# Starting the sparse stage with the blocks that need no key selection, and gating outputs out of PSUM

## The chip, the cores and the metric

The kernel runs on one core of one Trainium2 chip. The metric is device time in microseconds for one execution of the whole layer. TensorE (PE), VectorE (DVE), ScalarE (ACT), GpSimd (POOL) and the DMA queues, of which SyncE (SP) issues most, run at the same time, each through its own instruction stream in a fixed order, and wait for one another through semaphores. TensorE's granted clock stands at one of two levels, 1.2 or 2.4 GHz; a stretch's mean is given as a share of full speed.

## What is computed

One layer of a decoder over 1024 tokens of width 1024: a half-step feed-forward, two attention mixers side by side on the same normalised input, a gated merge, and a second half-step feed-forward. The part that matters here, cut from the reference:

```python
# (a) sparse attention, 128 queries at a time; top_k = 256
score = einsum('bths,bth->bts', relu(dots), wi)            # causal, else -inf
_, idx = lax.top_k(score, top_k)
logits = einsum('bthd,btkd->bthk', qa, kg) * HEAD_DIM**-0.5 # over the chosen keys
p = softmax(where(valid, logits, -inf))
y_a = einsum('bthc,hcd->bthd', einsum('bthk,btkc->bthc', p, vg), w_uv)
# (b) stick-breaking attention
log_a = log_sigmoid(z) + (reverse_cumsum(log_not) - log_not)
y_b = einsum('bhts,bshd->bthd', where(strict, exp(log_a), 0), v_b)
# merge
merged = sigmoid(g_a) * (y_a @ w_oA) + sigmoid(g_b) * (y_b @ w_oB)
x = x + merged @ w_out
```

A query block i of 128 tokens sees (i + 1) * 128 keys. Blocks 0 and 1 see at most 256, so every causal key is chosen there and no selection is made; blocks 2 to 7 need one.

## The kernel before, in words

Products are made in two parts, high and low, so that a product of full accuracy takes three matmuls (`mm3`), a logit or value product two or three. Between the two feed-forwards the order of the work is not written out: each piece is a generator (a stream) that yields what it needs next, an engine first, then tiles, rings of buffers or named marks. A planner (`Weave`) holds a cost for each instruction, picks the stream that can go earliest (a lower rank wins a tie), and so fixes the order of TensorE, VectorE, ScalarE and GpSimd. `when` says at which planned time a list of needs is fulfilled. SP's queue is ordered apart from it.

The stretch that the change touches is the planner's run named "attend". Its streams, with their ranks on TensorE: `values` (0), `sticks` (1), `head_values` (2), `latent_values` (3), `logits` (4), `outputs` (6), and the filling projections of gates that are left over (7). Also `topk`, one stream for the group of blocks 7, 2, 3 (mark `top0`) and one for 4, 5, 6 (mark `top1`): a bit-by-bit search for the 256th score, by signs counted on ScalarE, and then per block comparisons, a scan and a bias row of 0 and -1e30, stored by GpSimd into `bd`.

`sticks` makes the products `psz` of a head's query block, ScalarE two sigmoids, VectorE a scan (L1534) and a product (L1537). `values` turns them by transposes (`pstT`) copied out by ScalarE and VectorE (`turned_out`, L1581 and L1583), multiplies by the values (`psy`), and stores `y_b` (`ybhd`, `ybld`). At its end it waits for both marks `top0` and `top1`, closes the places `sw` and `ss` (the memory of scores and stick rows), and spawns `sparse`.

`sparse` opens the place `sc` there: three gate tiles, two more rows for `e`, six `o` tiles, and the value-up weight. It clears a raw tile on VectorE (L1657), loads the weight's eight heads through SP (L1660), and makes its high part on ScalarE (L1662) and its low part on GpSimd (L1664). The mark `c` says that the places are open, `uv` that the weight is there.

The sparse blocks go in the order `blocks = (5, 4, 7, 6, 3, 2, 1, 0)`. For each, `latent_queries` loads the queries through SP, `hidden_keys` loads the bias through SP (for blocks 0 and 1 GpSimd makes it), `logits` makes eight heads' products `psL` (L1723, L1724), VectorE adds the bias and takes the maximum (L1685, L1692), ScalarE the exponential (L1697), VectorE the normalising (L1699, L1700). The rows `e` lie in four tiles `a1`, two `left` and two `e`, taken in a fixed turn of eight heads. `latent_values` transposes four heads at a time (`pspT`, L1778) and multiplies by the latent values (`pso`, L1758 to L1760). `o_out` splits the result into two `o` tiles; `head_values` multiplies a pair of blocks by the value-up weight (`psya`), gives back its four `o` tiles, and marks `ya0` to `ya3`.

`outputs` projects: 16 units `ob` of y_b (eight weight pieces of 128 rows by two halves of the tokens), whose gated results go to `obd`, and eight units `oa` of y_a for tokens 512 to 1023, which add `obd` and go to `md`. A unit is twelve matmuls of 512 columns. For both, `gated` lets ScalarE copy the bank out (L1836), GpSimd multiply by the gate (L1841) and, for `oa`, add the other part (L1844), and GpSimd issue the store (L1845). `gate_load` loads the gate (L1828) and the other part (L1831) through SP, into a ring of three tiles; evictions share a ring `evr` of three.

After the run, the second half of the layer begins with the eight units `psm` for tokens 0 to 511, in new PSUM banks: VectorE multiplies by the gate out of PSUM (L1913), adds (L1914), and GpSimd makes low parts of weight pieces (L291) as it did in the run before (L962).

Of the kernel before, what the change touches and what calls it, by code (L numbers as in the profile page):

```python
# [93 lines left out]
class Weave:  # L94
# [94 lines left out]
    def when(self, needs, eng):  # L189
        t = 0.0  # L190
        for n in needs:
            if isinstance(n, str):
                t = max(t, self.when(self.marks[n], eng) if n in self.marks else float("inf"))
            elif isinstance(n, Stream):
                t = max(t, float("inf") if n.end is None else n.end)
            elif isinstance(n, (Ring, tuple)):
                ring, count = n if isinstance(n, tuple) else (n, 1)
                for old in ring.live[:max(len(ring.live) + count - ring.bufs, 0)]:
                    old = old.tensor.name
                    t = max(t, float("inf") if self.held[old] else self.done[old] + self.HOP)  # L200
            elif n is not None and not isinstance(n, (int, float)):
                t = max(t, self.ready[n.tensor.name] + self.hop(n.tensor.name, eng))
        return t
# [39 lines left out]
def trunk(ctx, tc, x, positions, g_ffn1, w1_gate, w1_up, w1_down, g_mix, w_in, g_cq, w_uq_a, w_q_idx,  # L243
# [664 lines left out]
    with fp as fpool, fps as fpsum, psm as psum, tc.manual_schedule(  # L908
# [271 lines left out]
        def heads():  # L1180
# [14 lines left out]
            for n, (nm, d) in enumerate((("kkh", kad[0]), ("kkl", kad[1]), ("kkh", vad[0]), ("kkl", vad[1]))):  # L1195
                yield SP, here[nm][n // 2]
                KV.append(here[nm][n // 2](nm))
                nc.sync.dma_start(f32(KV[-1]), d)
            mark("kv", *KV)

        def latent_queries():
            for n, i in enumerate(blocks):
                ring = here["qs"][n % 2]
                yield SP, "kv", ring
# [4 lines left out]
        blocks = (5, 4, 7, 6, 3, 2, 1, 0)  # L1209
# [304 lines left out]
        s = place("sw", "right")  # L1514
        here["x2"] = ring_of(s, "x2", 3, dt=F16)
# [107 lines left out]
        def values():  # L1623
# [18 lines left out]
            yield PE, *products, "top0", "top1"  # L1642
            yield PE, *outs
            s.close()
            keep.close()
            spawn(sparse())

        def sparse():
            c = here["c"] = place("sc", "right")
            here["gate"], here["e"] = ring_of(c, "gate", 3, (P, 512)), ring_of(c, "e", 2)  # L1650
            here["o"] = ring_of(c, "o", 6, dt=F32R)

            raw = here["e"]("uvraw")
            UV.extend((c("uvh", "uvh", 1, F32R), c("uvl", "uvl", 1, F32R)))
            mark("c")
            yield DVE
            nc.vector.memset(raw, 0.0)  # L1657
            for h in range(H):
                e = h % 2
                nc.sync.dma_start(raw[:, h * P + e * HD:h * P + (e + 1) * HD], w_uv_a[0, h])  # L1660
            yield ACT, raw
            nc.scalar.activation(UV[0], raw, AF.Copy)  # L1662
            yield POOL, raw, UV[0]
            nc.gpsimd.tensor_tensor(UV[1], raw, f32(UV[0]), op=ALU.subtract)  # L1664
            give(raw)
            mark("uv", UV[1])

        def hidden_keys():
            for b, i in enumerate(blocks):
                nk = (i + 1) * P  # L1670
                yield (SP if i >= 2 else POOL), biases, "top0", "top1"
# [30 lines left out]
        def logits():  # L1702
            n = 0
            yield PE, "sparse", "kv"
            kah, kal = KV[:2]
            for b, i in enumerate(blocks):
# [3 lines left out]
                for h in range(H):  # L1710
                    k = n % 8
                    if k > 5:
                        yield PE, "c"
                    ring = arings[1] if k < 4 else lefts if k < 6 else here["e"]
                    yield PE, ring
# [26 lines left out]
        def latent_products(b, g, pts, outs):  # L1742
            i = blocks[b]
            vah, val = KV[2:]
            if b % 2 == 0:
                yield PE, wbank, (here["o"], 2)
                OT[i // 2, g] = here["o"](f"oh{g}"), here["o"](f"ol{g}")
# [18 lines left out]
        def latent_values():  # L1766
            n, outs, products = 0, [], []
            yield PE, "c", "kv"
# [64 lines left out]
        def gated(ps, load, row, half, to):  # L1833
# [5 lines left out]
            gate, *other = here["gate", row, half]  # L1839
            yield POOL, o, gate  # L1840
            nc.gpsimd.tensor_tensor(o, o, gate, op=ALU.mult)  # L1841
            for t in other:
                yield POOL, o, t
                nc.gpsimd.tensor_tensor(o, o, t, op=ALU.add)  # L1844
            put_low(to, o)  # L1845
            give(o, gate, *other)

        def project(nm, rows, halves, outs):

            for d in range(0, ND, 2):  # L1850
# [3 lines left out]
                for e in range(2):  # L1854
                    for half in halves:
# [10 lines left out]
                        outs.append(spawn(gated(ps, coming, row, half, to)))  # L1866
                give(*W.parts)

        def outputs():
# [4 lines left out]
            yield SP, "uv"  # L1874
            for p in range(4):
                nc.sync.dma_start(f32(ybh[p]), ybd[0][p * P:(p + 1) * P, :])
                nc.sync.dma_start(f32(ybl[p]), ybd[1][p * P:(p + 1) * P, :])
            outs = []
            yield from project("ob", (ybh, ybl), range(2), outs)
            mark("obd", *outs)  # L1880
            yield PE, "ya1"
# [9 lines left out]
        here["c"].close()  # L1891
        rows_.close()
# [160 lines left out]
```

## Time and profile before

| what | value |
|---|---|
| median of 3 runs | 2324.99 us (2324.81 to 2325.76) |
| the profiled execution's own time | 2321.91 us |
| its span | 2320.1 us |
| TensorE busy, share of the span | 2190.6 us, 94% |
| VectorE | 1577.2 us, 68% |
| ScalarE | 1114.3 us, 48% |
| GpSimd | 901.1 us, 39% |

Busy times are those of instructions; a matmul's end is modelled and neighbouring matmuls overlap, so that the pace of matmuls is read from start to start. Stretches are told in microseconds from the span's start. The change lies between about 1240 and 1565 us.

### The profile page before, as it was taken

How to read it: one execution, taken by the hardware profiler on the slowest of the kernel's cores; microseconds unless marked ns; L12 is line 12 of the kernel's file. 1: busy time of each engine (PE TensorE's matmuls, PEld its weight loads, DVE VectorE, ACT ScalarE, POOL GpSimd, SP SyncE). 2: the span in 40 equal slices, each digit the busy share in tenths (PEclk: the TensorE clock that was granted, in tenths of full speed). 3: DMA queues.
4: the chain of work that ended last, by engine and by line, in shares of the span. 5: the costliest groups of instructions: out<-in, count | busy, mean ns of one | idle time of the engine just before them, and what ended most of it. 6: DMA issues, size and time to landing. Idle time of an engine off the chain costs nothing.

```text
span 2320.1 us, 30206 instructions
## 1 busy us (share of the span) xinstructions
PE 2190.6 (94%) x10460; PEld 1814.1 (78%) x10460; DVE 1577.2 (68%) x2497; ACT 1114.3 (48%) x2138; POOL 901.1 (39%) x659
## 2 busy tenths in 40 slices
PE   7999999999998999899898499989999999999999
PEld 6788888888888877777676388767878888888877
DVE  5766666688771698466788787833476666667685
ACT  4323233344462368998988365633332333233443
POOL 3555555332353344211111022266445555542233
PEclk9999999999999999999999699999999999999999
DMA  5233333587754433655455222457323333358755
GB/s 165 79 117 96 109 96 109 178 312 240 185 173 129 122 105 105 155 126 109 103 125 178 89 88 72 163 168 263 118 69 96 109 100 105 98 168 291 239 166 182
DMA packets 251497, 330.64 MB, mean 143 GB/s; under 512 B 19536, under 2 KB 154336, under 8 KB 251344
## 3 DMA queue, kind: packets, MB, share of 16 engines
q1 hardware_dynamic: 234224, 288.83, 41.4%
q0 software_dynamic: 7488, 24.16, 2.8%
q10 hardware_dynamic: 9632, 15.73, 2.0%
q8 instruction: 82, 1.34, 0.3%
q14 instruction: 71, 0.58, 0.1%
HBM read 234.78 MB, written 93.88 MB: 142 GB/s over the span
## 4 chain that ended last, share of the span: by engine, by line
PE 69%; DVE 10%; issue 7%; ACT 7%; DMA 4%; POOL 2%; ACTq 0%; SPq 0%; DVEq 0%; POOLq 0%
PE p L671 5%; PE p L672 5%; PE p L670 5%; PE pc L461 3%; PE pc L463 3%; PE pc L462 3%; PE pd L463 3%; PE pd L461 3%; PE pd L462 3%; PE pa L463 3%; PE pa L461 3%; PE pa L462 3%; ACT junka L1118 3%; PE pb L463 2%; PE pb L461 2%
## 5 line engine op out<-in xcount | busy, mean ns | idle before, releaser
L1118 ACT ACTIVATE junka<-u,cand,sig 128x1024 bf16<-128x1024 f32 (+5 forms) x186 | 182.5, 981 | 14.8 <-DVE cand L1115 4.7
L1534 DVE TENSOR_TENSOR_SCAN left<-left 128x640 f32<-128x640 f32 (+3 forms) x64 | 91.3, 1431 | 11.5 <-ACT left L1526 11.5
L1635 PE MATMUL pstT<-ident,sa 128*128 128x128 f32 x288 | 50.7, 292 | 25.8 <-DVE pt L1583 13.7
L1841 POOL TENSOR_TENSOR o<-o,gate 128x512 f32<-128x512 f32 x24 | 31.1, 1295 | 101.0 <-ACT o L1836 100.9
L1635 PEld LDWEIGHTS pstT<-ident,sa 128*128 128x128 f32 x288 | 36.4, 148 | 39.7 <-DVE pt L1583 21.3
L1602 POOL DMA_DIRECT2D ybld<-yl x16 | 8.8, 547 | 147.6 <-DVE yl L1600 122.0
L1583 DVE TENSOR_TENSOR pt<-pstT,pt 128x512 fp32r<-128x512 f32 (+1 forms) x96 | 51.2, 550 | 21.8 <-ACT pt L1581 21.4
L1723 PE MATMUL psL<-kkh,qs 128*128 128x512 f32 (+2 forms) x96 | 38.2, 404 | 25.1 <-DVE mx L1685 25.0
L1583 DVE TENSOR_TENSOR pt<-pspT,pt 128x512 fp32r<-128x512 f32 x72 | 46.4, 683 | 17.6 <-ACT pt L1581 17.6
L1447 DVE SCALAR_TENSOR_TENSOR u<-relu,WI,u 128x512 f32<-128x512 f32 (+1 forms) x70 | 51.9, 753 | 5.3 <-ACT relu L1440 3.9
L1697 ACT ACTIVATE e<-e,nm 128x768 f32<-128x768 f32 (+7 forms) x64 | 49.5, 776 | 12.0 <-DVE nm L1692 11.0
L671 PE MATMUL p<-bT,bS 128*128 128x512 f32 x132 | 51.8, 393 | 2.9 <-DVE bT L372 2.8
L1537 DVE TENSOR_TENSOR sa<-sa,left 128x639 f32<-128x639 f32 (+3 forms) x64 | 51.7, 811 | 3.0
L672 PE MATMUL p<-bT,bS 128*128 128x512 f32 x132 | 51.5, 393 | 1.0 <-POOL bS L372 1.0
L1581 ACT ACTIVATE pt<-pstT 128x512 fp32r<-128x512 f32 (+1 forms) x96 | 46.3, 501 | 12.0 <-PE pstT L1635 10.0
L671 PE MATMUL p<-aT,aS 128*128 128x512 f32 x132 | 51.4, 389 | 0.0
L1440 ACT ACTIVATE relu<-psdot 128x512 f32<-128x512 f32 (+1 forms) x80 | 40.9, 522 | 20.3 <-DVE u L1447 13.2
L1685 DVE CUSTOM_DVE_ANT_0 e<-psL,bias 128x512 f32<-128x512 f32 (+3 forms) x96 | 49.3, 549 | 2.0 <-PE psL L1724 1.9
L672 PE MATMUL p<-aT,aS 128*128 128x512 f32 x132 | 50.4, 389 | 0.0
L1581 ACT ACTIVATE pt<-pspT 128x512 fp32r<-128x512 f32 x72 | 39.3, 594 | 22.2 <-PE pspT L1778 22.1
L1526 ACT ACTIVATE left<-psz 128x512 f32<-128x512 f32 (+2 forms) x96 | 45.5, 497 | 7.6 <-ACT evg L1051 2.5
L1528 ACT ACTIVATE sa<-psz 128x512 f32<-128x512 f32 (+2 forms) x96 | 45.8, 507 | 2.1 <-ACT evg L1051 1.5
(3057 smaller groups left out, 8312.3 us busy)
## 6 DMA issues: line engine op xcount, KB each, us to landing
aw<-in_w_down_dram SPq DMA_DIRECT2D x33, 512.0 KB, 4.9
bw<-in_w_down_dram SPq DMA_DIRECT2D x33, 512.0 KB, 4.9
a0r<-in_w_gate_dram SPq DMA_DIRECT2D x22, 512.0 KB, 4.1
a1r<-in_w_up_dram SPq DMA_DIRECT2D x22, 512.0 KB, 4.9
b0r<-in_w_gate_dram SPq DMA_DIRECT2D x22, 512.0 KB, 4.1
b1r<-in_w_up_dram SPq DMA_DIRECT2D x22, 512.0 KB, 5.0
x<-in_x_dram SPq DMA_DIRECT2D x16, 512.0 KB, 6.2
gd<-evg ACTq DMA_DIRECT2D x32, 256.0 KB, 2.6
```

The lines of the kernel that those rows point to most:

```text
L461: nc.tensor.matmul(ps, a[:, c], b[k][:, HI], start=start and k == 0, stop=False, skip_group_check=True)
L462: nc.tensor.matmul(ps, a[:, c], b[k][:, LO], start=False, stop=False, skip_group_check=True)
L463: nc.tensor.matmul(ps, a[:, l], b[k][:, HI], start=False, stop=k == 3, skip_group_check=True)
L670: nc.tensor.matmul(ps[q][m], S[:, h], T[:, HI], start=p == 0, stop=False)
L671: nc.tensor.matmul(ps[q][m], S[:, h], T[:, LO], start=False, stop=False)
L672: nc.tensor.matmul(ps[q][m], S[:, l], T[:, HI], start=False, stop=p == last)
L1118: nc.scalar.activation(junks[1][:, 0:(i + 1) * P], score[i], AF.Sign, scale=sig[:, b:b + 1], bias=cand.bitcast(F32)[:, b:b + 1], accum_out ...
L1447: nc.vector.scalar_tensor_tensor(ac, r, wv, ac, op0=ALU.mult, op1=ALU.add)
L1534: nc.vector.tensor_tensor_scan(back, back, back, 1.0, op0=ALU.mult, op1=ALU.bypass)
L1581: nc.scalar.activation(pt[:, off:512], tp[:, off:512], AF.Copy)
L1583: nc.vector.tensor_sub(pt[:, 512 + off:1024], tp[:, off:512], f32(pt[:, off:512]))
L1635: nc.tensor.transpose(tp[:, q * P:(q + 1) * P], A[n + q][:, j * P:(j + 1) * P], ident)
```

## The change

The order of the blocks becomes (1, 0, 5, 4, 7, 6, 3, 2). `hidden_keys` waits for no selection where the block needs none, and otherwise for its own group's mark alone. The queries wait for the mark `ka2`, set when the two key tiles are issued, where they waited for all four key and value tiles.

The places open in two parts. The ring `x2` of the selection moves from `sw` into a place `sx` of its own, so that `sw` can be closed as soon as `values` is through; four of the six `o` tiles open then (`sc`, mark `o`). The rest (`sd`: gates, two rows `e`, two `o` tiles, the value-up weight; mark `c`) opens as before, when both selections are done. The raw value-up weight goes through two gate tiles in halves, cleared on GpSimd.

A logit row takes whichever ring is free first by the plan, among `a1`, `left` and, once it is there, `e`; a list among the needs means the earliest of its members. The loads of y_b wait for `o` in place of `uv`; the projections' start waits for `c`, and `oa` for `ya2` in place of `ya1`.

For `oa` a new function `merged` takes the place of `gated`: VectorE multiplies the bank by the gate and adds the other part; the bank and the gate are given back after the multiply. `ob` keeps `gated`.

```diff
@@ when
+            elif isinstance(n, list):
+                t = max(t, min(self.when((one,), eng) for one in n))
@@ heads, latent_queries
+                if n == 1:
+                    mark("ka2", *KV)
             mark("kv", *KV)
...
-                yield SP, "kv", ring
+                yield SP, "ka2", ring
...
-        blocks = (5, 4, 7, 6, 3, 2, 1, 0)
+        blocks = (1, 0, 5, 4, 7, 6, 3, 2)
@@ attend
-        s = place("sw", "right")
-        here["x2"] = ring_of(s, "x2", 3, dt=F16)
+        chosen, s = place("sx", "right"), place("sw", "right")
+        here["x2"] = ring_of(chosen, "x2", 3, dt=F16)
@@ values
-            yield PE, *products, "top0", "top1"
+            yield PE, *products
             yield PE, *outs
             s.close()
+            outputs_of.extend((place("sc", "left"), None))
+            mark("o")
+            yield PE, "top0", "top1"
+            chosen.close()
             keep.close()
             spawn(sparse())
 
+        outputs_of = []
+
+        def output_place(name, tag, bufs, dt, shape):
+
+            n = here["outputs"] = here.get("outputs", -1) + 1
+            c, bufs = (outputs_of[0], 4) if n % 6 < 4 else (outputs_of[1], 2)
+            return c(name, tag, bufs, dt, shape)
+
+        oring = ring_of(output_place, "o", 6, dt=F32R)
+
         def sparse():
-            c = here["c"] = place("sc", "right")
+            c = here["c"] = outputs_of[1] = place("sd", "right")
             here["gate"], here["e"] = ring_of(c, "gate", 3, (P, 512)), ring_of(c, "e", 2)
-            here["o"] = ring_of(c, "o", 6, dt=F32R)
-
-            raw = here["e"]("uvraw")
+
             UV.extend((c("uvh", "uvh", 1, F32R), c("uvl", "uvl", 1, F32R)))
+            raws = [here["gate"]("uvraw") for half in range(2)]
             mark("c")
-            yield DVE
-            nc.vector.memset(raw, 0.0)
...
+            yield POOL
+            for half, raw in enumerate(raws):
+                nc.gpsimd.memset(raw, 0.0)
+                for h in range(4):
+                    nc.sync.dma_start(raw[:, h * P + h % 2 * HD:h * P + (h % 2 + 1) * HD], w_uv_a[0, 4 * half + h])
...
@@ hidden_keys
-                yield (SP if i >= 2 else POOL), biases, "top0", "top1"
+                yield (SP if i >= 2 else POOL), biases, None if i < 2 else "top0" if i in groups[0] else "top1"
@@ logits
-            yield PE, "sparse", "kv"
+            yield PE, "sparse", "ka2"
...
-                    k = n % 8
-                    if k > 5:
-                        yield PE, "c"
-                    ring = arings[1] if k < 4 else lefts if k < 6 else here["e"]
-                    yield PE, ring
+                    rings = [arings[1], lefts] + ([here["e"]] if "e" in here else [])
+                    yield PE, rings
+                    ring = min(rings, key=lambda r: weave.when((r,), PE))
@@ latent_products, latent_values
-                yield PE, wbank, (here["o"], 2)
-                OT[i // 2, g] = here["o"](f"oh{g}"), here["o"](f"ol{g}")
+                yield PE, wbank, (oring, 2), "c" if b else None
+                OT[i // 2, g] = oring(f"oh{g}"), oring(f"ol{g}")
...
-            yield PE, "c", "kv"
+            yield PE, "o", "kv"
@@ gated keeps only the gate's multiply; new beside it
+        def merged(ps, load, row, half, to):
+            yield DVE, ps, evr, load
+            gate, other = here["gate", row, half]
+            yield DVE, ps, evr, gate
+            o = f32(evr("o"))
+            nc.vector.tensor_tensor(o, ps, gate, op=ALU.mult)
+            give(ps, gate)
+            yield DVE, o, other
+            nc.vector.tensor_tensor(o, o, other, op=ALU.add)
+            yield POOL, o
+            put_low(to, o)
+            give(o, other)
@@ project, outputs
-                        outs.append(spawn(gated(ps, coming, row, half, to)))
+                        outs.append(spawn((merged if nm == "oa" else gated)(ps, coming, row, half, to)))
...
-            yield SP, "uv"
+            yield SP, "o"
...
+            yield PE, "c"
             outs = []
...
-            yield PE, "ya1"
+            yield PE, "ya2"
```

## Rows read from the trace of the kernel before

**Rows 1.** The page's head: the span and its instructions.
```profile
span 2320.1 us, 30206 instructions
```

**Rows 2.** Stretches by limiter: busy time (instructions) of each engine, granted clock, DMA.
```profile
core 0: us, PE busy (x) PEld busy (x) DVE busy (x) ACT busy (x) POOL busy (x), PEclk, DMA share, GB/s
1260.00:1290.70 30.70, 15.82 (x69) 11.39 (x69) 27.65 (x55) 22.24 (x48) 3.98 (x4) 0.73 0.31 99
1290.70:1314.40 23.70, 7.37 (x24) 5.34 (x22) 21.62 (x40) 4.13 (x8) 2.22 (x4) 0.50 0.32 97
1314.40:1337.50 23.10, 11.36 (x41) 8.00 (x42) 14.33 (x53) 9.40 (x17) 2.88 (x2) 0.69 0.25 78
1337.50:1531.30 193.80, 188.57 (x1035) 160.26 (x1033) 145.74 (x437) 114.85 (x249) 61.74 (x56) 1.00 0.36 116
1531.30:1540.30 9.00, 0.11 (x1) 0.00 (x0) 0.00 (x0) 1.63 (x2) 7.20 (x6) 0.62 0.66 219
1540.30:1563.80 23.50, 23.46 (x96) 19.33 (x97) 15.69 (x17) 6.36 (x9) 11.41 (x10) 0.93 0.47 150
```

**Rows 3.** Waits, 1200 to 1620 us: waiter <- waited for: total, times, longest.
```profile
PE psL L1723 <- DVE mx L1685: 25.0, 4, 17.7
...
ACT uvh L1662 <- DMA uvraw<-in_w_uv_a_dram: 22.4, 1, 22.4
...
ACT o L1836 <- DMA md<-o: 10.6, 2, 7.4
...
PE psm L302 <- ACT o L1836: 8.9, 1, 8.9
```

**Rows 4.** VectorE in order of time: last stick, selection's end, first normalised row.
```profile
1290.00 0.68 DVE L1537 TENSOR_TENSOR sa<-sa,left 128x511 f32<-128x511 f32 x1
...
1313.99 0.39 DVE L1174 TENSOR_SCALAR cum<-gt 128x896 bf16<-128x896 f16 x1
...
1327.34 0.62 DVE L1700 TENSOR_SCALAR e<-e,ri 128x768 f32<-128x768 f32 x1
```

**Rows 5.** VectorE in order of time: the operations of blocks 1 and 0.
```profile
1488.41 0.41 DVE L1685 CUSTOM_DVE_ANT_0 e<-psL,bias 128x256 f32<-128x256 f32 x1
...
1489.70 0.15 DVE L1699 RECIPROCAL ri<-ssum 128x1 f32<-128x1 f32 x1
1489.89 0.35 DVE L1700 TENSOR_SCALAR e<-e,ri 128x256 f32<-128x256 f32 x1
1490.36 0.69 DVE L1739 TENSOR_TENSOR ol<-pso,oh 128x512 fp32r<-128x512 f32 x1
...
1493.94 0.41 DVE L1819 TENSOR_TENSOR yal<-psya,yah 128x256 fp32r<-128x256 f32 x1
...
1496.58 0.21 DVE L1692 TENSOR_SCALAR nm<-mx 128x1 f32<-128x1 f32 x1
```

**Rows 6.** TensorE in order of time: transposes, and starts of neighbouring matmuls of 256 and 512 columns.
```profile
1471.86 1.04 PE L1778 MATMUL pspT<-ident,e 128*128 128x128 f32 x8
...
1490.21 0.28 PE L1723 MATMUL psL<-kkh,qs 128*128 128x256 f32 x1
1490.33 0.28 PE L1724 MATMUL psL<-kkl,qs 128*128 128x256 f32 x1
...
1493.23 0.39 PE L1760 MATMUL pso<-pt,kkh 128*128 128x512 f32 x1
1493.46 0.40 PE L1758 MATMUL pso<-pt,kkh 128*128 128x512 f32 x1
```

**Rows 7.** GpSimd's gate multiply, gate loads' landing, and VectorE beside a GpSimd subtraction.
```profile
L1841 POOL TENSOR_TENSOR o<-o,gate x24: 1265/1285/1414, 1345.4 to 1543.9; 128x512 f32<-128x512 f32 x24
...
DMA to landing us min/median/max: 2.6/3.1/7.3
...
1548.44 0.68 DVE L1913 TENSOR_TENSOR gate<-gate,psm 128x512 f32<-128x512 f32 x1
1549.15 2.62 DVE L1914 TENSOR_TENSOR gate<-gate 128x512 f32<-128x512 f32 x1
...
1548.84 2.39 POOL L291 TENSOR_TENSOR woa4l<-woa4r,woa4h 128x1024 fp32r<-128x1024 f32 x1 [1.38 <-ACT woa4h L289]
```

More of the change, by code (lines that the diff above doesn't have):

```diff
@@ L1640, in values @@
                 n += 4
[L1642 removed]
+            yield PE, *products
             yield PE, *outs
             s.close()
+            outputs_of.extend((place("sc", "left"), None))
+            mark("o")
+            yield PE, "top0", "top1"
+            chosen.close()
             keep.close()
             spawn(sparse())
+        outputs_of = []
[4 more added lines that the diff above has]
+        oring = ring_of(output_place, "o", 6, dt=F32R)
         def sparse():
[L1649 removed]
+            c = here["c"] = outputs_of[1] = place("sd", "right")
             here["gate"], here["e"] = ring_of(c, "gate", 3, (P, 512)), ring_of(c, "e", 2)
[L1651 to L1653 removed]
             UV.extend((c("uvh", "uvh", 1, F32R), c("uvl", "uvl", 1, F32R)))
+            raws = [here["gate"]("uvraw") for half in range(2)]
             mark("c")
[L1656 to L1665 removed]
+            yield POOL
[3 more added lines that the diff above has]
+                    nc.sync.dma_start(raw[:, h * P + h % 2 * HD:h * P + (h % 2 + 1) * HD], w_uv_a[0, 4 * half + h])
+            for half, raw in enumerate(raws):
+                cols = slice(half * 512, half * 512 + 512)
+                yield ACT, raw
+                nc.scalar.activation(UV[0][:, cols], raw, AF.Copy)
+                yield POOL, raw, UV[0]
+                nc.gpsimd.tensor_tensor(UV[1][:, cols], raw, f32(UV[0][:, cols]), op=ALU.subtract)
+                give(raw)
             mark("uv", UV[1])
@@ L1838, in gated @@
             yield POOL, o, load
-            gate, *other = here["gate", row, half]
+            gate, = here["gate", row, half]
             yield POOL, o, gate
             nc.gpsimd.tensor_tensor(o, o, gate, op=ALU.mult)
-            for t in other:
-                yield POOL, o, t
-                nc.gpsimd.tensor_tensor(o, o, t, op=ALU.add)
             put_low(to, o)
-            give(o, gate, *other)
+            give(o, gate)
+        def merged(ps, load, row, half, to):
[10 more added lines that the diff above has]
+            give(o, other)
         def project(nm, rows, halves, outs):
@@ L1891, in trunk @@
         here["c"].close()
+        outputs_of[0].close()
         rows_.close()
```

## The prediction

> **What bounds the kernel now.** The change touches one stretch of a 2320.1 us span: the end of the stick-breaking heads, the sparse blocks, and the output projections [rows 1]. I read the busy table over that stretch first, cut where the limiter changes [rows 2]. Four stretches matter.
>
> From 1260.0 to 1314.4 us VectorE is the limit: 27.65 of 30.70 us and then 21.62 of 23.70 us busy, while TensorE does 15.82 and then 7.37 us at a granted clock of 0.73 and 0.50. What VectorE does there is the last scans of the sticks, the copies of their transposes, and the second key selection (blocks 4, 5, 6). The sticks' last product starts at 1290.00 and the selection's last operation at 1313.99 [rows 4].
>
> From 1314.4 to 1337.5 the sparse stage starts up: TensorE is busy 11.36 of 23.10 us at clock 0.69, VectorE only 14.33. The waits say why [rows 3]: the logit products stood 17.7 us at the longest for VectorE's maxima (three logit banks fill, and VectorE is still selecting), and ScalarE stood 22.4 us on the load of the raw value-up weight, which its queue has ahead of the first exponentials. The first normalised row comes only at 1327.34 [rows 4].
>
> From 1337.5 to 1531.3 TensorE is the limit: 188.57 of 193.80 us at full clock, with VectorE at 145.74. All sparse blocks and all projection units lie in it. From 1531.3 to 1540.3 TensorE does 0.11 us: it waits 8.9 us for the last eviction, which itself waited for an `md` store [rows 3], because GpSimd (7.20 of 9.00 us busy) is behind with two operations per `oa` unit. After 1540.3 TensorE is full again (23.46 of 23.50).
>
> So the stage's end is: when TensorE becomes saturated, plus the TensorE work left then, plus the closing gap.
>
> **The work that moves.** Blocks 1 and 0 need no selection, so their logits wait for the sticks (1290.7) and no longer stand last. Their TensorE work, at the start-to-start pace of matmuls in one run [rows 6]: 16 heads x 2 logit matmuls of 256 columns at 0.12 us is 3.8; 24 transposes at 1.04/8 us is 3.1; 6 groups x 3 value matmuls at 0.23 us is 4.1; 24 head-value matmuls of 256 columns at 0.12 us is 2.9. Together 14 us, which leave a saturated stretch for one where TensorE stands mostly idle.
>
> Their VectorE work at 256 wide [rows 5]: per head 0.41 (bias and maximum), 0.21, 0.15 and 0.35, so 1.12 us, times 16 is 17.9; six transposed copies and four latent outputs, both 512 wide, at 0.69 are 6.9; four head outputs at 0.41 are 1.6. That is 26 us at most; half of the heads are 128 wide, so I take 20. This is the catch: it goes into the stretch where VectorE is the limit, with only 2.1 us idle between 1290.7 and 1314.4 [rows 2]. The planner serves ready VectorE jobs by their ready time, so logits and selection steps alternate, and the second selection ends later by what it lets in front. Below: 4 us, if the small blocks fill only idle time and wait otherwise. Above: all 20 less 2.1 idle, 18 us. I take 12, as their own chain (logit, exponential, normalise, transpose, with six rows available before the later places open) spreads past the selection's end. The selection then ends near 1326.
>
> **The start-up that goes.** After the selection, block 5 and 4 find the exponential table loaded, ScalarE isn't parked on the weight by an earlier place in its queue (the two halves come through the gate ring, cleared on GpSimd: between nothing and 1.29 us each, the multiply in [rows 7] being the nearest row), and the `ob` units are queued right behind, their matmuls needing only `ybh`, `ybl` and weights. SP still issues the eight weight loads, and two of its three gate places are held by the halves until GpSimd has subtracted them, so the first `ob` gates come a few us later than the `ob` matmuls; two banks and three evictions give 5 units x 2.74 us of cover (12 matmuls x 0.23). Saturation came 23.1 us after the selection's end; nothing saved would leave all of it, projections at once would leave 0. The 12.9 us from the selection's end to the first normalised row are those of the parked weight, the table and the closing of the old places; of the other 10.2, the filling of the pipeline, the projection units should cover half. I take 5. So saturation at 1331 in place of 1337.5.
>
> **The saturated stretch.** 193.8 less 14 is 179.8 us. I add 3 for small-block work that is not through by 1331 and 1 for the output ring: blocks 5 and 4's second group must wait until the first pair's four tiles are given back, which needs the value-up weight. The last `oa` matmul then ends at 1331 + 183.8 = 1514.8 in place of 1531.3: **16.5 us earlier**.
>
> **The `oa` units.** Removed per unit: a ScalarE eviction and two GpSimd operations of 1.29 us (8 x 2.57 is 20.6 us of GpSimd). Added on VectorE: a multiply out of PSUM, as the row of 0.68 us, and an add of two SBUF operands; 8 x 1.4 is 11 us, which VectorE has room for in a stretch where it is busy 75% and loses 20. The closing gap of 9.0 us should shrink to the last gate's lateness plus one multiply, 3 us: **6 us earlier**.
>
> Against it: the bank is now freed only when the gate has landed, a median 3.1 us after its issue [rows 7]. With three places and two tiles a unit, a gate is issued when the add two units back is done. Through three units that is two landings (6.2) plus two adds or multiplies (1.4) and issue, 7.9 us, 2.6 a unit, against 2.74 on TensorE: just hidden when nothing else stands in SP's queue. Below 0, above 8 x 2 us if each weight piece in that queue delays one; I take **2 us later**. `md` stores stay on GpSimd.
>
> An add of two SBUF operands took 2.62 us where GpSimd's 2.39 us subtraction started 0.3 us before it [rows 7]; four such subtractions fall among the eight new adds. The Trainium skill ("SBUF — State Buffer", Who interferes with whom) says that a VectorE instruction with two SBUF inputs and a GpSimd instruction that reads SBUF exclude each other for the whole instruction. The row agrees: by the rule four adds would stretch by 1.9 us, 7.7 in all, and the gain would be 13 in place of 20 were none of it hidden. By the row's neighbour, the multiply out of PSUM at 0.68 beside the same work, nothing is lost. VectorE at 8 x 0.68 + 4 x 0.69 + 4 x 2.62 = 18.7 us for 22 us of TensorE still keeps up, so the sum has no term of its own for it.
>
> **Sum.** 16.5 + 6 - 2 = 20.5, say 20 us. The profiled execution took 2321.9 us (span 2320.1), 3.1 below the median of 2325.0 of the runs shown; I take the saving from the median: **2305.0 us**.
>
> **Rivals.**
> *The hole is filled almost wholly.* The small blocks let the selection pass (4 us later, 1318) and the projections saturate TensorE at 1321: the last `oa` matmul at 1500.8, 30.5 earlier, and 8 off the closing gap: 2286.5. For it: `ob` matmuls need nothing of the selection. Against it: the planner opens their places only after it, and VectorE's idle time there is 2.1 us.
> *The hole only moves.* All of the small blocks' VectorE work stands before the selection's end (1333), start-up stays at 9 us: saturation 1342, the end 1524.8, 6.5 earlier; 4 off the gap and 4 lost on gates: 2318.5. For it: VectorE's 91% busy time. Against it: 14 us of TensorE work are gone from the saturated stretch in any case.
> *Slower: the gates pace `oa`.* If SP's queue lets a unit's two loads go only after the unit before has added, each unit costs 3.1 + 0.3 + 0.68 + 0.69 to 2.62, so 4.8 to 6.7 us, and block 3 and 2's VectorE work queues behind the waiting multiply. It decides where a unit exceeds 2.74 + 22.5/8 = 5.6 us. At 6.7 the stage loses 32 against a gain of 22.5: 2334. For it: one landing took 7.3 us. Against it: three places let a gate run ahead.
> *The order on VectorE stays.* If the planner puts the small blocks' logits behind the whole selection, they are worked off in the start-up: half of their 20 us of VectorE work stands ahead of block 5's, TensorE saturates at 1347.5, the last `oa` matmul ends at 1347.5 + 180.8 = 1528.3, 3 us earlier, and the closing gap's gain goes to the gates: 2322, within 0.2%.
>
> **Chances.** Forecast 0.54 (its own range 2294 to 2314), filled wholly 0.12, moved 0.19, slower 0.10, order unchanged 0.05. Within 0.2% (4.6 us) is about what a measurement of this kernel can't tell from no change. Faster takes the first three but for the upper end of "moved": 0.82; same 0.08; slower 0.10. The range 2286 to 2320 holds the forecast, half of the wholly filled case and nearly all of the moved one, near 0.8.
>
> **What would show it.** Exponentials 256 wide right after 1291; the second selection's last store between 1318 and 1333; logit products of block 5 without a 17 us wait; TensorE full from about 1331 for about 184 us; no GpSimd adds into `o`; a gap of about 3 us ahead of `psm`. The prediction is wrong if the selection slides beyond 1335, if TensorE has holes behind `oa` multiplies waiting for gates, or if the value-up weight holds up the output ring of blocks 5 and 4.

## The result, and the profile after

The changed kernel took 2309.3 us (median of 4 runs, 2307.02 to 2310.65) beside 2325.4 us for the kernel before in the same job: a ratio of 0.9934, with a 95% interval of 0.9922 to 0.9946. It is 16.1 us faster; the forecast was 20. The profiled execution took 2307.02 us, with a span of 2305.2. Every time below is a median of runs that agree within 0.6%, but for one slow run of 2820.0 us of the first kernel with the projections early, which its ratio leaves out.

The size is near the forecast, but the terms it is made of are others. Milestones of the two profiled executions, in us from the span's start:

| | before | after | earlier by |
|---|---|---|---|
| last stick product | 1290.0 | 1289.6 | 0.4 |
| second selection's last operation ends | 1314.4 | 1332.9 | -18.5 |
| first `ob` matmul | 1338.3 | 1331.4 | 6.9 |
| block 5's first logits | 1298.7 | 1345.7 | -47.0 |
| last `oa` matmul | 1531.4 | 1530.0 | 1.4 |
| first `psm` matmul | 1540.3 | 1530.9 | 9.5 |
| first `wout010l` matmul | 1591.6 | 1577.9 | 13.7 |
| span | 2320.1 | 2305.2 | 14.9 |

The stretches of after, with the columns of [rows 2], cut where its own limiter changes:

```profile
1290.70:1314.40 23.70, 13.14 (x55) 9.96 (x53) 21.39 (x78) 12.01 (x32) 1.64 (x3) 0.72 0.35 96
1314.40:1333.00 18.60, 12.38 (x42) 8.38 (x42) 17.89 (x53) 6.66 (x19) 0.54 (x1) 0.68 0.18 59
...
1330.50:1346.40 15.90, 15.83 (x63) 12.81 (x63) 2.92 (x6) 4.98 (x8) 6.29 (x7) 0.88 0.33 98
1346.40:1515.90 169.50, 165.87 (x901) 138.38 (x900) 145.50 (x404) 100.28 (x204) 44.76 (x41) 1.00 0.37 123
1515.90:1530.80 14.90, 10.70 (x49) 8.50 (x47) 5.12 (x10) 3.34 (x6) 3.94 (x4) 0.89 0.71 228
1530.80:1553.00 22.20, 22.15 (x98) 18.38 (x99) 16.21 (x20) 7.68 (x11) 11.52 (x6) 1.00 0.42 131
```

TensorE now works in the selection stretch (13.14 us of 23.70, before 7.37), is full from 1330.5 as forecast, and the dead stretch of 9 us ahead of `psm` is gone. But VectorE does 2.92 of 15.90 us after the selection, and a new hole stands among the `oa` units, 1515.9 to 1530.8. Such a hole, behind `oa` multiplies that wait for gates, is one of the prediction's own signs of being wrong.

The first of these is seen in VectorE's timeline of after, from the selection's last operation to block 5's first maximum (start, duration, line, operation, idle time before it and what ended it):

```profile
1332.48 0.39 DVE L1176 TENSOR_SCALAR cum<-gt 128x896 bf16<-128x896 f16 x1
1332.79 0.68 DVE L1756 TENSOR_TENSOR ol<-pso,oh 128x512 fp32r<-128x512 f32 x1
1346.38 0.69 DVE L1704 CUSTOM_DVE_ANT_0 e<-psL,bias 128x512 f32<-128x512 f32 x1 [12.91 <-PE psL L1741]
```

VectorE waits 12.91 us for block 5's logits. They come late because 57 `ob` matmuls, nearly five units, stand ahead of them in TensorE's queue (1331.4 to 1345.7). In before, block 5's logits were the first work after the sticks.

The hole, in the timelines of VectorE and then of SP's queue of after:

```profile
1520.08 0.69 DVE L1867 TENSOR_TENSOR o<-psoa,gate 128x512 f32<-128x512 f32 x1 [2.50 <-DMA gate<-gd]
```

```profile
1513.44 0.38 SPq L959 DMA_DIRECT2D woa2r<-in_w_o_a_dram  x1
1514.53 0.32 SPq L1845 DMA_DIRECT2D gate<-gd  x1
1515.13 0.32 SPq L1848 DMA_DIRECT2D other<-obd  x1
1515.87 0.32 SPq L1845 DMA_DIRECT2D gate<-gd  x1
```

The loads go in turn, a gate and an `other` for each unit. The multiply at 1520.08 is the sixth of eight, and its gate is the one issued at 1514.53: it is there only 5.5 us later (the median landing of after's gates is 3.6), and a weight piece was issued 1.1 us before it. The bank is held until the multiply (L1867) has read it. TensorE's waits of after in that stretch (line, releaser, total, times, longest):

```profile
PE psya L304 <- DVE o L1867: 2.3, 1, 2.3
PE psya L304 <- DVE yal L1836: 1.0, 1, 1.0
PE psm L304 <- DVE o L1867: 0.9, 1, 0.9
```

Two of them are for the multiply. The wait of 1.0 us is for a copy of the head values (`yal`), which itself stood for ScalarE's copy (`yah`), not for a gate.

**A ledger of TensorE.** From 1290 to the first `psm` matmul both kernels do the same matmuls. Each counted at its full-speed pace [rows 6] (0.23 us for 512 columns, 0.12 for 256, 0.13 for a transpose; 0.17 for the few of 384), the groups of both traces add up to 202.7 us. What the span from 1290 to `psm` holds beyond that is TensorE time lost to waits and to the lower clock level: 250.3 - 202.7 = 47.6 us before, 240.9 - 202.7 = 38.2 after. The 9.4 us between them are the 9.5 by which `psm` comes earlier. Transposes follow each other at 0.11 us in the long runs of both traces, so every lost time is some 6 us too low; the differences stand. The figure is given for the experiments below; it sees nothing of what happens behind the first `psm` matmul.

### The profile page after: what moved, and what is told of

It reads as the page before. It is cut to its first block, busy times and chain, and to the rows that moved or that the text cites. A ratio compares the mean times of both kernels' runs of the same rounds, so it can differ in the third digit from the quotient of the medians.

```text
span 2305.2 us, 30193 instructions
## 1 busy us (share of the span) xinstructions
PE 2194.1 (95%) x10460; PEld 1813.5 (79%) x10460; DVE 1580.9 (69%) x2512; ACT 1112.6 (48%) x2131; POOL 882.9 (38%) x646
## 4 chain that ended last, share of the span: by engine, by line
PE 67%; DVE 12%; ACT 9%; issue 5%; DMA 5%; POOL 1%; ACTq 1%; SPq 0%; DVEq 0%; POOLq 0%
PE p L673 5%; PE p L674 5%; PE p L672 5%; PE pc L463 3%; PE pc L464 3%; PE pc L465 3%; ACT junka L1120 3%; PE pd L465 3%; PE pd L463 3%; PE pd L464 3%; PE pa L463 3%; PE pa L465 3%; PE pa L464 3%; PE pb L463 2%; PE pb L465 2%
## 5 line engine op out<-in xcount | busy, mean ns | idle before, releaser
L1587 DVE TENSOR_TENSOR pt<-pstT,pt 128x512 fp32r<-128x512 f32 (+1 forms) x96 | 51.3, 551 | 21.7 <-ACT pt L1585 21.2
L1716 ACT ACTIVATE e<-e,nm 128x256 f32<-128x256 f32 (+7 forms) x64 | 49.5, 775 | 24.1 <-DVE nm L1711 23.7
L1795 PE MATMUL pspT<-ident,e 128*128 128x128 f32 x288 | 41.8, 283 | 14.1 <-DVE e L1719 14.1
L1795 PEld LDWEIGHTS pspT<-ident,e 128*128 128x128 f32 x288 | 35.0, 144 | 21.3 <-DVE e L1719 12.4
```

Source lines behind the costliest of these rows:

```text
L1587: nc.vector.tensor_sub(pt[:, 512 + off:1024], tp[:, off:512], f32(pt[:, off:512]))
L1795: nc.tensor.transpose(tp[:, q * P:(q + 1) * P], E[n + q][:, j * P:(j + 1) * P], ident)
```

## The experiments

Twelve runs, in three jobs on three chips, each job with its own runs of the kernel before (2323.9, 2326.5 and 2323.7 us); between jobs the ratios to these are compared. The position of the last stick product varies by itself from 1288 to 1293 between profiled executions, so that a milestone alone is good to 2 or 3 us.

### Each half of the name alone

First, only `merged`, put into the kernel before:

```diff
+        def merged(ps, load, row, half, to):
...
-                        outs.append(spawn(gated(ps, coming, row, half, to)))
+                        outs.append(spawn((merged if nm == "oa" else gated)(ps, coming, row, half, to)))
```

> The kernel before, with the function merged for the oa units and nothing else of the change: blocks in the old order, places opened at once. Theory A (the gain of the change lies in the end of the stage: the gap ahead of psm fell from 9.0 to 0.9 us, and the next stretch gave some 5 us more, while the last oa matmul came only 1.4 us earlier): 2310 to 2315 us, with a gap ahead of psm under 3 us. Theory B (the prediction's sizes: 16.5 us from the blocks' order, 4 from the oa units): 2319 to 2323 us.

Measured: 2318.4 us, ratio 0.9974 (0.9963 to 0.9984), lost time 44.5 us, with sticks that ended 3.3 us later than in before. The median lies between the ranges of the two theories. The gap ahead of `psm` fell from 8.9 us [rows 3] to 0.9:

```profile
PE psm L302 <- DVE o L1853: 0.9, 1, 0.9
```

So the closing gap was GpSimd's backlog, as the prediction read it.

Second, the changed kernel with the `gated` of before for `oa`, so that order and places alone are left:

```diff
-                        outs.append(spawn((merged if nm == "oa" else gated)(ps, coming, row, half, to)))
+                        outs.append(spawn(gated(ps, coming, row, half, to)))
```

> The changed kernel with the oa units evicted by ScalarE and gated on GpSimd, as before the change. Theory A: the last oa matmul a few us ahead of 1531 or level with it, the gap ahead of psm again near 9 us, 2320 to 2325 us. Theory B: the last oa matmul 10 to 16 us earlier than before, 2309 to 2315 us.

Measured: 2308.6 us, ratio 0.9931 (0.9919 to 0.9943), lost time 34.3 us: no difference from the whole change in the total. Two things cancel. The last `oa` matmul ends at 1525.6, 4.4 us earlier than with `merged`, with no hole in the `oa` units:

```profile
1515.90:1527.00 11.10, 9.62 (x45) 7.51 (x43) 1.09 (x3) 4.46 (x7) 9.48 (x10) 1.00 0.64 215
1527.00:1549.00 22.00, 21.64 (x94) 17.59 (x95) 16.14 (x17) 6.70 (x9) 15.00 (x10) 1.00 0.55 187
```

and the gap ahead of `psm` is 1.5 us without VectorE's help: the eight units are spread over 34.4 us (1491.2 to 1525.6) where before they took 29.0, which would give GpSimd the time (argued from the spread, not shown by an edit). Behind `psm` GpSimd still carries two units (15.00 us busy of 22.00, after 11.52 of 22.20), and TensorE waits 2.9, 0.4 and 0.3 us for its low parts there (in after 2.3 us for the first of these, none for the others). Whatever closes that gap first takes the gain; the two halves don't add.

### What the selection's lateness costs

The last steps of the second group's selection get rank 0 on VectorE:

```diff
+            first = (0,) if gi else ()
...
-                yield DVE
+                yield DVE, *first
```

> The changed kernel with the last steps of the second selection (comparisons, scan, bias rows) given the first place on VectorE wherever they are ready, so that the small blocks' operations no longer push them back. The selection should end at 1315 to 1320 us in place of 1332.9. Theory A (TensorE's work up to its saturation decides, and the small blocks' part then comes after it): 2302 to 2310 us. Theory B (each us of the selection's end is a us of the stage): 2291 to 2297 us.

Measured: 2306.1 us, ratio 0.9922 (0.991 to 0.9934), lost time 37.3 us (`psm` at 1530.0). The selection ended at 1323.0, not as early as expected, and block 5's logits came at 1335.0, 10.7 us earlier than in after. All that gave 2 to 3 us by the ratio, within the intervals: the `ob` units cover TensorE until block 5 is ready, so a late selection is not itself the price. A theory that put most of the missing time on it falls. The last `oa` matmul ended at 1527.7, 2.2 us earlier than in after, but the gap ahead of `psm` was 2.3 us in place of 0.9.

### The projections earlier

The projections no longer wait for the mark of the second places; only the gate loads do:

```diff
-            yield PE, "c"
             outs = []
...
+            yield SP, "c"
             yield SP, (here["gate"], 1 + ob)
```

> The changed kernel with the ob units free to start before the last places open (their gate loads wait for the places, their matmuls don't). Theory A: up to five units, 13.7 us of TensorE work at full clock, move into the stretch from 1305 to 1331 where TensorE is about half idle, 2297 to 2303 us. Rival: their banks and eviction tiles, held until the gates come, stand in the way of the last stick outputs and small blocks, and what is won there is lost behind it: 2308 us or more.

Measured: 2301.6 us, ratio 0.9897 (0.9883 to 0.9912), lost time 28.9 us. The first `ob` matmul stands at 1321.8. TensorE in the selection's stretch, in windows of 10 us from 1310 to 1330:

```profile
1310.00:1320.00 10.00, 5.38 (x22) 4.25 (x22) 9.58 (x31) 3.86 (x13) 0.00 (x0) 0.83 0.00 0
1320.00:1330.00 10.00, 9.18 (x44) 7.34 (x45) 9.40 (x28) 4.98 (x15) 0.54 (x1) 1.00 0.33 111
```

Against 4.53 us at a clock of 0.71 for after in the same 1320 to 1330. Run once more beside the changed kernel itself on one chip:

> The changed kernel, unedited, on the same chip as the three others of this group, as their yardstick. Theory P (what gains is that the places open in two parts, so that the projections of y_b fill VectorE's selection stretch; the block order itself costs about as much as it brings): 2307 to 2311, some 5 above the kernel with the old block order in the group before. Rival Q (the lead of the old block order there was a difference between chips or days): 2303 to 2305.

> The changed kernel with the projections not behind the mark of the second places, once more, beside the changed kernel on the same chip. Theory P: 2299 to 2304, some 6 below it, since the first projection comes 10 us earlier, in VectorE's selection stretch. Rival Q: within 2 of it.

Measured: the changed kernel 2308.2 us (0.9936, 0.9924 to 0.9949; lost time 38.2), with the projections early 2304.2 us (0.9914, 0.9901 to 0.9928; lost time 30.8). So the gain is there, and nearer to 4 than to 8 us.

The edits of the two sections above at once:

```diff
-                yield DVE
+                yield DVE, *first
...
-            yield PE, "c"
...
+            yield SP, "c"
```

> The changed kernel with the second selection first on VectorE and the ob units free to start before the last places open, both together. Theory C: the projections already fill the hole, so the earlier selection adds little to the 8 us of the early projections: 2298 to 2302 us. Theory B (each us of the selection's end counts): 2290 to 2295 us.

Measured: 2305.7 us, 0.9909 (0.9893 to 0.9924), lost time 37.1 us, outside both ranges. The planner put the first `ob` matmul at 1331.2 again, so this run doesn't have the effect it was made to combine.

The early projections with the gating of before:

```diff
-            yield PE, "c"
...
+            yield SP, "c"
...
-                        outs.append(spawn((merged if nm == "oa" else gated)(ps, coming, row, half, to)))
+                        outs.append(spawn(gated(ps, coming, row, half, to)))
```

> The ob units free to start early, and the oa units gated on GpSimd as before the change. Theory C (the gap ahead of psm closes by the projections' earlier start alone, so the gating on VectorE brings nothing on top): 2299 to 2303 us, level with the early projections. Rival (VectorE's gating is worth 6 us as predicted): 2306 to 2309 us.

Measured: 2309.2 us, 0.9925 (0.9911 to 0.9939), lost time 30.8 us. The last `oa` matmul ended at 1522.0, near the 1520.6 of the early projections with `merged`, but `psm` took 26.1 us (1523.5 to 1549.6) in place of 22.1: TensorE waits there 1.4 us for a low part from GpSimd and 0.5 for a high part from ScalarE, and its clock is 0.93 over that stretch, 1.00 with `merged`. Here GpSimd's backlog came out behind the gap. By the ratios `merged` is worth 3 to 7 us in this order, beside the two runs of the early projections, the lower figure within the intervals. Its worth hangs on the order of the rest.

### The hole among the `oa` units

Each `oa` unit loads only its gate, which is also what is added; the stick-breaking half is left out of the output. The bank is still held by the gate:

```diff
-            yield SP, (here["gate"], 1 + ob)
+            yield SP, here["gate"]
...
-                nc.sync.dma_start(tiles[1], obd[r * P:(r + 1) * P, cols])
```

> The changed kernel in which an oa unit loads the gate alone and uses it for the add too (the other part is left out, so the result lacks the stick-breaking half of these tokens): one load and one ring place a unit in place of two. Theory E (the hole of some 4 us among the oa units, 1516 to 1531, is a bank held until its gate lands): no wait of TensorE above 1 us there, the last oa matmul near 1525, 2303 to 2307 us. Rival: the hole is the head values' chain of copies, and stays: 2308 to 2311 us.

Measured: 2305.0 us, ratio 0.9906 (0.9892 to 0.9921), lost time 33.9 us. The hole's stretch in this kernel:

```profile
1515.90:1525.80 9.90, 9.59 (x50) 7.55 (x48) 4.48 (x10) 2.71 (x6) 4.29 (x4) 1.00 0.69 222
```

With three gates ahead, TensorE is full at full clock, and the last `oa` matmul ends at 1525.7, 4.3 us earlier. The hole of after is the bank held for a late gate, and it costs 4 us. The edit takes a load and a tile off each unit at once, so it doesn't tell whether the ring's places or the landing made the gate late.

### The block order

The changed kernel with the old order of the blocks; the places in two parts and `merged` stay:

```diff
-        blocks = (1, 0, 5, 4, 7, 6, 3, 2)
+        blocks = (5, 4, 7, 6, 3, 2, 1, 0)
...
-            yield PE, "ya2"
+            yield PE, "ya1"
```

> The changed kernel with the blocks in the old order (5, 4, 7, 6, 3, 2, 1, 0), and oa behind the pair that is second in it; the places still open in two parts and oa is still gated out of PSUM. Theory C (after the first four runs: what counts is TensorE work done in the stretch between the sticks and the selection's end, and an earlier start of the projections; both come from the blocks' order): near the first run, 2315 to 2320 us. Rival D (opening the places in two parts, and the weight no longer parked on ScalarE, give most): 2306 to 2311 us.

Measured: 2303.4 us, ratio 0.9903 (0.9889 to 0.9917), lost time 34.5 us. This was the miss that changed the reading: both theories had it slower than it was, and the old order came out faster than the new one. The selection ends at 1315.3 again, and the first `ob` matmul stands at 1299.9.

That left one part of the change that the kernels so far had in common. The next has nothing but it: the old order, the old gating, and the places opened in two parts.

```diff
-        blocks = (1, 0, 5, 4, 7, 6, 3, 2)
+        blocks = (5, 4, 7, 6, 3, 2, 1, 0)
...
-                        outs.append(spawn((merged if nm == "oa" else gated)(ps, coming, row, half, to)))
+                        outs.append(spawn(gated(ps, coming, row, half, to)))
...
-            yield PE, "ya2"
+            yield PE, "ya1"
```

> The places in two parts, with the old block order and with oa gated by ScalarE and GpSimd as before, so that neither half of the change's name is in it. Theory P: 2303 to 2310, first projection of y_b near 1300 and the last oa matmul near 1523, as with the old order and VectorE's gating. Rival U (order and gating bring the gain, the places only allow it): 2318 to 2326. Rival V (the places bring about half, and gating on VectorE the rest): 2309 to 2314, with a closing gap of some 5 to 9 us ahead of psm.

Measured: 2300.6 us (2295.81 to 2301.95), ratio 0.9898 (0.9885 to 0.9912), lost time 28.9 us. That is below every range written down for it. All of its runs lie below all of the changed kernel's on the same chip (2306.45 to 2312.02): it is 7.6 us faster than the whole change, and 23 faster than before. Its windows of 10 us from 1290 to 1350:

```profile
1290.00:1300.00 10.00, 6.88 (x27) 5.46 (x28) 9.72 (x24) 3.57 (x7) 0.53 (x1) 0.65 0.13 27
1300.00:1310.00 10.00, 2.66 (x7) 1.53 (x6) 8.48 (x15) 0.68 (x2) 1.69 (x3) 0.69 0.54 167
1310.00:1320.00 10.00, 10.00 (x38) 7.74 (x37) 7.02 (x18) 0.55 (x1) 1.53 (x3) 0.80 0.31 98
1320.00:1330.00 10.00, 6.36 (x24) 5.24 (x24) 4.67 (x12) 6.96 (x12) 7.44 (x7) 0.83 0.52 139
1330.00:1340.00 10.00, 9.38 (x48) 7.61 (x47) 9.89 (x23) 6.00 (x12) 8.21 (x9) 1.00 0.74 242
1340.00:1350.00 10.00, 10.00 (x55) 8.41 (x54) 7.08 (x17) 5.07 (x11) 2.38 (x3) 1.00 0.56 186
```

TensorE is full from 1310 to 1320, mostly with `ob`. The last operation of the selection and the first of these matmuls, which wait for the stored y_b:

```profile
1313.44 0.39 DVE L1176 TENSOR_SCALAR cum<-gt 128x896 bf16<-128x896 f16 x1
```

```profile
1298.26 0.44 PE L304 MATMUL psob<-ybh,ob0h 128*128 128x512 f32 x1
...
1306.90 0.80 PE L304 MATMUL psob<-ybh,ob0h 128*128 128x512 f32 x1 [6.34 <-DMA ybh<-ybhd]
```

So the selection ends at 1313.8, near the 1314.4 of before and 19 us earlier than in after. By then TensorE has done no more than in after: counted as in the ledger, 7.9 us of work by 1314, beside 7.7 in after and 3.9 in before. The gain is in the start-up behind the selection: 16.9 us of work from 1314 to 1337.5, beside 10.7 and 7.0.

The `oa` units end at 1514.6, ahead of the last head values, and TensorE's only waits from 1510 to 1532 are these:

```profile
PE pso L1775 <- ACT pt L1585: 1.0, 1, 1.0
PE psm L304 <- DVE yal L1836: 0.9, 1, 0.9
PE psya L304 <- DVE yal L1836: 0.3, 1, 0.3
```

The small blocks, still last, now stand between the `oa` units and `psm` and give GpSimd 7 us for its backlog: no gap, with the gating of before.

Last, the old order with `merged` and with the projections not behind the second mark:

```diff
-        blocks = (1, 0, 5, 4, 7, 6, 3, 2)
+        blocks = (5, 4, 7, 6, 3, 2, 1, 0)
...
+            yield SP, "c"
...
-            yield PE, "c"
...
-            yield PE, "ya2"
+            yield PE, "ya1"
```

> The old block order with the projections not behind the mark of the second places (only the gate loads are). Theory P: the projections started at 1299.9 there already, held then by their own loads, so that nothing is left to gain: 2301 to 2306. Rival W (the mark still holds the projections back between 1300 and 1325): first projection before 1298, TensorE above 7 us of 10 from 1300 on, 2296 to 2300.

Measured: 2303.9 us, ratio 0.9916 (0.9903 to 0.993), lost time 34.2 us, first `ob` matmul at 1299.3: nothing to gain, as expected. The three kernels with the old order lie at 2300.6 to 2303.9 us with intervals that overlap; they aren't told apart here.

## Why the prediction came out near, and where its steps failed

**The step that failed: the 14 us of the moved blocks.** The prediction took 14 us of small-block work off the saturated stretch and put 3 back for what would not be through by 1331: 11 net, as if nothing of the sparse blocks had been done ahead of it in before. The matmuls of before from 1290 to 1337.5, by line and form (count, busy us, mean ns):

```profile
L1723 PE MATMUL psL<-kkh,qs 128*128 128x512 f32 x8 | 4.9, 607 | 0.3 <-DVE mx L1685 0.3
L1724 PE MATMUL psL<-kkl,qs 128*128 128x512 f32 x8 | 4.6, 570 | 0.0
L1723 PE MATMUL psL<-kkh,qs 128*128 128x256 f32 x8 | 3.8, 472 | 23.8 <-DVE mx L1685 23.7
L1724 PE MATMUL psL<-kkl,qs 128*128 128x256 f32 x8 | 3.0, 376 | 0.0
...
L1778 PE MATMUL pspT<-ident,e 128*128 128x128 f32 x9 | 1.4, 278 | 0.0
...
L1758 PE MATMUL pso<-pt,kkh 128*128 128x512 f32 x2 | 0.9, 449 | 0.2 <-ACT pt L1581 0.2
L1760 PE MATMUL pso<-pt,kkh 128*128 128x512 f32 x2 | 0.9, 446 | 0.7 <-DVE pt L1583 0.7
L1759 PE MATMUL pso<-pt,kkl 128*128 128x512 f32 x2 | 0.8, 394 | 0.0
```

That is all of block 5's logits, nine transposes and six value products: 16 x 0.23 + 16 x 0.12 + 9 x 0.13 + 6 x 0.23 = 8.2 us at full speed. And those of after from 1290 to 1330.5:

```profile
L1795 PE MATMUL pspT<-ident,e 128*128 128x128 f32 x24 | 7.5, 405 | 14.1 <-DVE e L1719 14.1
L1740 PE MATMUL psL<-kkh,qs 128*128 128x256 f32 x16 | 6.7, 421 | 0.6 <-DVE mx L1704 0.6
L1741 PE MATMUL psL<-kkl,qs 128*128 128x256 f32 x16 | 5.8, 364 | 0.0
L1775 PE MATMUL pso<-pt,kkh 128*128 128x512 f32 x6 | 3.6, 595 | 1.0 <-ACT pt L1585 1.0
L1776 PE MATMUL pso<-pt,kkl 128*128 128x512 f32 x6 | 3.1, 518 | 0.0
L1777 PE MATMUL pso<-pt,kkh 128*128 128x512 f32 x5 | 2.7, 534 | 0.0
```

24 x 0.13 + 32 x 0.12 + 17 x 0.23 = 10.9 us, so the small blocks' own part was sized right. Block 5's was left out: the credit is 10.9 - 8.2 = 2.7 us, not 11. The small blocks didn't fill an empty stretch, they took block 5's place in it.

**The losses behind saturation.** For these the prediction added 1 (the output ring) and 2 (the gates). Counted by the ledger, after needs 199.5 us (1330.5 to 1530.0) for 189.3 us of work, so it loses 10.2, where before lost 1.8 (192.0 of 193.8). By stretches: 1.9 from 1330.5 to 1346.4, where the `ob` units begin at the lower clock level (mean 0.88); 2.4 up to 1515.9; and 5.9 in the hole up to 1530.0, of which 3.3 are the first two waits shown above and some 2 the lower clock level (mean 0.89; the matmuls from 1520.9 to 1525.7 take 4.8 us for 2.8 us of work). So 193.8 - 2.7 + 8.4 = 199.5, where the forecast had 193.8 - 11 + 1 = 183.8 and 2 for the gates: the last `oa` matmul ends 1.4 us earlier in place of 14.5 (16.5 - 2). Block 5's work left out makes 8.3 of that difference, the losses 5.4. The one-load kernel shows the hole's share, 4.3 us of the milestone.

**Saturation, right in time by two errors.** 1331 was forecast, 1330.5 measured, and the `ob` matmuls, queued behind the small blocks, need nothing of the selection, as the prediction said. But its sum took the selection's end at 1326 and 5 us of start-up. Measured, the selection ended 6.9 us later than that, and saturation came 2.4 us ahead of its end, with the `ob` units alone and without block 5. That the two cancel is luck.

**Right.** The closing gap: 6 forecast, 8.0 measured (8.9 to 0.9), and `merged` alone shows that GpSimd's backlog made it, even if the spread of the units closes it as well. That the gates pace `oa` only a little: 2 forecast, about 4 measured, far from the 32 of the slower rival; the sign of the hole, though, did come.

**The selection.** Its end was forecast at 1326 within 1318 to 1333; it came at 1332.9, at the upper end. The small blocks' VectorE groups from 1289.5 to 1333 add up to 24.1 us, without the head outputs that come later, where the prediction took 20 of at most 26 with them: the short operations per head (0.21, 0.15 and 0.08 us) don't shrink with the row. That end of the range was the mark of the rival in which the hole only moves; 10 us of it, given back, were worth 2 to 3 us, within the intervals.

**What stood in no term.** Behind the first `psm` matmul another 4.2 us are won up to `wout010l` (51.3 us before, 47.0 after). Before began `psm` at the lower clock level (0.93 over its stretch [rows 2], after 1.00), so that it took 23.7 us in place of 22.0, and waited 1.2 and 3.0 us for GpSimd's low parts of the next weights, in place of 2.3. That a closed gap alone gives this back is not shown: of the kernels with the gating of before and a gap of 0.9 to 1.5 us, places alone takes 47.1 us (1521.6 to 1568.7), order alone 49.0, and the early projections 53.3.

**How the sum came near.** Forecast 16.5 + 6 - 2 = 20.5; measured 1.4 + 8.0 + 4.2 = 13.6 up to `wout010l`, 14.9 in span, 16.1 between medians. The first term was too large by 13 with the gates, and two others too small by 6, so that the total is near by luck. The direction was argued from a cause that holds (TensorE works while VectorE selects), but the wrong work was credited for it: the kernel with the places in two parts and the old order leaves the selection where it was and fills the start-up behind it, with `ob` units and block 5 together. By 1350 the ledger has 23.8 us of work done before, 31.1 after, and 37.7 there.

**The rule on VectorE's adds.** None of the eight was stretched: 0.68 to 0.69 us each. Two met a GpSimd subtraction, and both had begun first. The first of them in the timelines of after, VectorE's add and then GpSimd's subtraction, with one that met no add below it:

```profile
1500.01 0.68 DVE L1870 TENSOR_TENSOR o<-o,other 128x512 f32<-128x512 f32 x1
```

```profile
1500.08 2.87 POOL L964 TENSOR_TENSOR oa4l<-oa4r,oa4h 128x1024 fp32r<-128x1024 f32 x1 [34.00 <-ACT oa4h L962]
...
1511.01 2.41 POOL L964 TENSOR_TENSOR oa6l<-oa6r,oa6h 128x1024 fp32r<-128x1024 f32 x1
```

Here it was GpSimd that took 2.87 in place of 2.41 us, and 2.71 beside the last add. The Trainium skill ("SBUF — State Buffer", Who interferes with whom) says that the instruction that issues first holds the shared ports and the other one is blocked; both cases agree with it, and the 2.62 us row of [rows 7] is the other order of the same pair. The prediction's 7.7 us would have needed four adds to come second. That none did lies in this kernel's order: in the other kernels with `merged` 14 adds began while such a subtraction ran, and each ended 0.54 to 0.56 us after it, 0.71 to 2.80 us long. With the selection first there were three among the eight (2.50, 1.47 and 2.70 us); the first, with the subtraction below it:

```profile
1505.63 2.50 DVE L1871 TENSOR_TENSOR o<-o,other 128x512 f32<-128x512 f32 x1
```

```profile
1505.19 2.39 POOL L964 TENSOR_TENSOR oa4l<-oa4r,oa4h 128x1024 fp32r<-128x1024 f32 x1 [1.25 <-ACT oa4h L962]
```

What they cost that kernel in time is not shown.

**What stays open.** The places in two parts hold several edits (y_b's loads behind the earlier mark, the value-up weight through two gate tiles, the free choice of a row's ring, the queries behind two tiles, a block's bias behind its own group's mark). They were not run apart; that y_b's loads set the first `ob` matmul is seen in its wait of 6.34 us, not shown by an edit. A version of `merged` without the hole that leaves no work out wasn't run.

## What to carry to other kernels

Before crediting work that is moved into a hole, count what already runs in the hole: the gain is the difference of the two, and work that depends on nothing there (here the `ob` projections) leaves its length as it is, where work that competes for the engine that is the limit makes it longer (the selection ended at 1313.8 with the one, at 1332.9 with the other). Count an engine's work at full pace from a fixed point to the milestone and subtract it from the time: the lost time of each version shows where it won, but only up to that milestone (the early projections with the gating of before had lost 30.8 us there and took 2309.2 us all the same). And when a change has a name with two halves, run what is left with both halves taken out; here that was the part that gained, and it has the lowest median of the study.

## What was not expected of the hardware

Two short waits cost TensorE more than their length: the hole holds 3.3 us of waits and 5.9 us of lost time. In after those of 1.0 and 2.3 us ahead of `psya` (1517.6 and 1520.9) were followed by matmuls at the lower of the two levels (1.2 GHz): from 1521.94 on those of 256 columns follow each other at 0.21 us in place of 0.12, and those of 512 columns at 0.43 in place of 0.23 until 1525.4. Its timeline:

```profile
1520.92 0.35 PE L304 MATMUL psya<-oh,uvh 128*128 128x256 f32 x1 [2.30 <-DVE o L1867]
...
1521.94 0.45 PE L304 MATMUL psya<-oh,uvh 128*128 128x256 f32 x1
1522.19 0.41 PE L305 MATMUL psya<-ol,uvh 128*128 128x256 f32 x1
...
1524.96 0.63 PE L305 MATMUL psoa<-yal,oa6h 128*128 128x512 f32 x1
1525.39 0.46 PE L306 MATMUL psoa<-yah,oa6l 128*128 128x512 f32 x1
```

In the one-load kernel, without these waits, the same stretch has a granted clock of 1.00; and with the order alone, a single wait of 1.5 us ahead of `psm` was followed by a stretch at 1.00 too.
